# Two loads on a second queue at the head, one projection moved, and the last store in two parts

## The chip, the cores and the metric

The kernel runs as one program on one core of a Trainium2 chip. The metric is the device time of one execution in microseconds, and the trace is one profiled execution. A core has five engines that run at once, each through its own list of instructions in order: TensorE (PE in the rows, with its weight loads as PEld), VectorE (DVE), ScalarE (ACT), GpSimd (POOL) and SyncE (SP). A "q" behind a name (SPq) is the engine's sequencer, which issues the DMAs that stand in its list. The engines meet through semaphores.

## What is computed

One inference step of a one-layer hybrid encoder in fp32: 512 prompt rows and 32 sample rows of width 1024. One projection feeds three attention groups: A (chunk band with a bias), B (an indexer scores the keys, the best k are picked, attention runs over those) and M (256 memory rows).

```python
def _mixer_inputs(x, g, w_in, pos):
    z = _rmsnorm(x, g) @ w_in
    qa, ka, va, ga, qb, kb, vb, gb, qm, gm, qi, ki, wi = _split_cols(z)
...
def _merge(x, oa, ob, om, ga, gb, gm, w_out):
    o = jnp.concatenate([oa * jax.nn.silu(ga), ob * jax.nn.silu(gb), om * jax.nn.silu(gm)], axis=-1)
    return x + o @ w_out
...
y_prompt = _rmsnorm(xp, norm_final_g)
```

The columns `qi`, `ki` and `wi` (8 x 32, 32 and 8 columns: 296 together) are the indexer's queries, key and weights. The keys, values and indexer keys are outputs too.

## The kernel before

**Number form.** A prompt product is made of three fp32r products: an operand is split in a rounded part (`...h`) and the rest (`...l`), and h·h, h·l and l·h are summed in a PSUM bank. The rounded part of a weight is made by ScalarE (`rounded`), the rest by VectorE or GpSimd (`tsub`); for x the two are `xTh` (ScalarE) and `xTl` (VectorE), both scaled with the norm's weights `g_mix`. Products for the 32 sample rows take the weights as loaded (`raw`) and plain fp32 (`xF`).

**Stages.** The head is the index group: for each of 8 K tiles (128 rows of the contraction) one tile of x transposed (`xr`, 272 KB) and one tile of the 296 index columns of `w_in` (`raw`, 148 KB) are loaded, split, and multiplied (`index_group`: nine products a K tile, three token tiles each in three forms). After it come small products for the sample (`bank<-raw,xF`, which for `ka` needs all four of the 384 KB pieces of `ka`'s weights), the first key tile (`bank<-xr,gw`), and then the projections `EARLY` and `LATE` in the order of those lists, while the indexer, the picks and the attention units run between them. The end is the output projection, whose last tile is the fourth prompt tile: a squared sum, a power on GpSimd (`run`), a scale on ScalarE (columns 0 to 511) and on VectorE (columns 512 to 1023), and one store of 512 KB (`settle`).

**What sets the order.** Nothing is scheduled by hand. A planner (`Line`) is run while the kernel is written: it keeps a modelled clock per engine, costs every instruction, and starts the next step of that coroutine whose data it holds to be there. Its numbers (DMA rate by `rate`, `lag`, margins) thus set the order of the instructions on every engine. While the model says that TensorE would wait during the index group, `warm` writes filler products (`bank<-ones`, 128x128, whose result nobody reads). Every instruction of the kernel is written through one helper, so nearly all rows of the trace bear the line 405, and tiles are told apart by name.

**Names that the change touches.** `x_load` issues the loads of x and of the index weights on SP's queue. `w_split` splits the weights; `WV` lists the weight pieces (0 to 3 are the index weights, 4 to 7 those of `ka`) whose low part VectorE makes. `EARLY` orders the projections. `settle` ends a tile.

Of the kernel before, what the change touches and what calls it, by code (L numbers as in the profile page):

```python
# [10 lines left out]
F32 = mybir.dt.float32  # L11
F32R = mybir.dt.float32r
BF16 = mybir.dt.bfloat16
AF = mybir.ActivationFunctionType
ALU = mybir.AluOpType
# [3 lines left out]
P = 128  # L19
# [3 lines left out]
D = 1024  # L23
# [3 lines left out]
NT = S // P  # L27
# [8 lines left out]
WV = (0, 1, 2, 3)  # L36
# [8 lines left out]
EARLY = ("ka", "va", "mk", "mv", "qa0", "qa1", "ga0", "qa2", "ga1", "ga2", "qm0", "gm0", "qm1", "gm1")  # L45
# [15 lines left out]
class Free:  # L61


    eng = None
# [26 lines left out]

class Line:
# [4 lines left out]
    def __init__(self):  # L97
        self.clk = {"PE": 1.35, "DVE": 0.7, "ACT": 0.9, "POOL": 1.2, "SP": 0.7}
# [57 lines left out]
    @staticmethod  # L156
    def lag(of, to):

        if of is None and to == "PE":
            return 0.3  # L160
        if of == to or of is None:
            return 0.127 if to == "DVE" else 0.09 if to == "POOL" else 0.0
        return 0.95 if of == "SP" else 0.26 if to == "PE" else 0.2 if of == "PE" else 0.06 if of == "POOL" else 0.15
# [68 lines left out]
    def rate(self):  # L232

        t = self.clk["SP"]
        return 340e3 if t < 1 else 170e3 if t < 2.3 else 330e3 if t < 7 else 380e3

    def op(self, eng, op, outs, ins, kw):
# [16 lines left out]
        d = (outs[0].size() * 4 / self.rate() if eng == "SP" else  # L254
# [33 lines left out]
    def begin(self, o, t):  # L288
        last = self.last
        o.start = t  # L290
        if o.eng == "SP":
            o.end = max(t + 1.3, last["DMA"]) + o.d
            o.after = {"SP": t + 0.45, "DMA": o.end}
        else:
            d = o.d
            if o.eng == "PE":
                (self.window, self.busy, self.over, self.slow) = last["array"]
                d = self.array(t, d)
# [7 lines left out]
        self.clk[o.eng] = o.end if o.eng != "SP" else t  # L306
# [127 lines left out]
def hybrid_step(ctx: ExitStack, tc: tile.TileContext, a: dict):  # L434
    ctx.enter_context(tc.manual_schedule())
    nc = tc.nc
    line = Line()
    V, G, A, PE, DMA = (Timed(line, n, e) for n, e in (("DVE", nc.vector), ("POOL", nc.gpsimd), ("ACT", nc.scalar),
                                                       ("PE", nc.tensor), ("SP", nc.sync)))

# [94 lines left out]
    def rounded(out, in_, scale=1.0):  # L535
        A.activation(out, in_, AF.Copy, scale=scale)
# [94 lines left out]
    def w_split():  # L631
        at = {}
        for i in range(len(w_list)):
# [26 lines left out]
            if i < 4:  # L660
                for kk in range(2):
                    yield line.at(raw[:, kk, :])
                    rounded(wh[:, kk, :], raw[:, kk, :])
# [141 lines left out]
    def x_load():  # L805
# [8 lines left out]
        for kk in range(2):  # L814
# [4 lines left out]
            DMA.dma_start(raw[:, kk, :], w_in[rows, QI:QI + 296])  # L819
# [1184 lines left out]
    gf = sq = ss = None  # L2004

    def final():

        nonlocal gf, sq, ss
# [6 lines left out]
        ss = fp.tile([P, NT + 1, 8], F32, name="ss")  # L2015
        ready.append(True)
# [5 lines left out]
    def settle(t, c0, n):  # L2022
# [30 lines left out]
        A.activation(y[:rows, 0:512], y[:rows, 0:512], AF.Copy, scale=run)  # L2053
        V.scalar_tensor_tensor(y[:rows, 512:D], y[:rows, 512:D], run, gf[:rows, 512:D], op0=ALU.mult, op1=ALU.mult)
        DMA.dma_start(a["y_prompt"][t * P:(t + 1) * P, :] if t < NT else a["y_sample"], y)
# [70 lines left out]
```

## Time and profile before

| | us |
|---|---|
| median of 3 runs | 353.21 (352.42 to 353.29) |
| the profiled execution, whole | 352.53 |
| its span, first to last instruction | 350.8 |
| TensorE busy in it | 342.6 (98%) |
| VectorE, ScalarE, GpSimd busy | 277.5, 224.2, 174.3 |
| TensorE's granted clock, mean | 0.996 of full speed |

The span is what the rows cover; 1.73 us of the profiled execution lie around it. Times in the rows are microseconds from the span's start. Busy time of TensorE is taken from starts that the profiler saw and ends that it modelled: matmuls overlap in the rows, so the time of a step is read from one start to the next.

### The profile page before, as it was taken

Reading aid. Unit: us, or ns where it says so; the run is one execution under the profiler, and the core shown is the slowest. Engines: PE = TensorE matmul, PEld = TensorE weight load, DVE = VectorE, ACT = ScalarE, POOL = GpSimd, SP = SyncE. Lnnn points to the kernel's source line nnn. Section 1 sums busy time; section 2 is a strip of 40 time slices with the busy share of each in tenths; the row PEclk is TensorE's granted clock in tenths of the full one; section 3 lists DMA queues with packets and bytes.
Section 4 is the critical chain, followed back from the end, with each engine's and each line's share of the span. In section 5 each row is a group of like instructions: output and inputs, shape, how many; then the busy total and the mean of one; then the engine's idle time right before and its main releaser. Section 6 shows DMA issues by size and latency. Waiting matters only on the chain.

```text
span 350.8 us, 7580 instructions
## 1 busy us (share of the span) xinstructions
PE 342.6 (98%) x2748; PEld 300.2 (86%) x2748; DVE 277.5 (79%) x700; ACT 224.2 (64%) x536; POOL 174.3 (50%) x195
## 2 busy tenths in 40 slices
PE   8999999999999999999999999999999999999992
PEld 8979989989999998898898899899986777676882
DVE  3765768699889999997999945798996899674743
ACT  5759678898564876894757427413795786472542
POOL 3468264475554585255634473744471465215622
PEclk9999999999999999999999999999999999999998
DMA  7999542456538251343231232232372537300033
GB/s 230 323 360 354 134 140 75 143 162 152 151 92 296 66 144 39 78 127 88 76 91 45 93 124 58 60 93 98 95 284 92 180 106 265 114 0 2 0 111 143
DMA packets 39604, 46.31 MB, mean 132 GB/s; under 512 B 5360, under 2 KB 32624, under 8 KB 39568
## 3 DMA queue, kind: packets, MB, share of 16 engines
q1 hardware_dynamic: 39568, 45.85, 42.0%
q8 instruction: 21, 0.34, 0.4%
q14 instruction: 15, 0.12, 0.1%
HBM read 39.67 MB, written 6.16 MB: 131 GB/s over the span
## 4 chain that ended last, share of the span: by engine, by line
PE 95%; DVE 1%; ACT 1%; issue 1%; POOLq 0%; POOL 0%; ACTq 0%; DVEq 0%
PE bank L405 95%; DVE rot L405 1%; DVE xr L405 0%; ACT junkS L405 0%; DVE rt L405 0%; ACT wh L405 0%; ACT sq L405 0%; POOLq L2114 0%; POOL xr L405 0%; ACT bf_ok L405 0%; ACT k L405 0%; POOL ss L405 0%; ACT wI L405 0%; DVE ones L405 0%; ACTq L405 0%
## 5 line engine op out<-in xcount | busy, mean ns | idle before, releaser
L405 POOL TENSOR_TENSOR wl<-raw,wh 128x512 fp32r<-128x512 f32 (+1 forms) x69 | 104.5, 1523 | 79.9 <-ACT wh L405 68.2
L405 ACT ACTIVATE wh<-raw 128x512 fp32r<-128x512 f32 (+2 forms) x77 | 50.7, 662 | 23.4 <-PE bank L405 12.0
L405 PE MATMUL bank<-wh,xTh 128*128 128x384 f32 (+1 forms) x184 | 61.2, 347 | 0.2 <-ACT k L405 0.2
L405 PE MATMUL bank<-wl,xTh 128*128 128x384 f32 (+1 forms) x184 | 58.8, 334 | 0.0
L405 PE MATMUL bank<-wh,xTl 128*128 128x384 f32 (+1 forms) x184 | 58.5, 332 | 0.0
L405 ACT ACTIVATE z<-z,st 128x256 f32<-128x256 f32 (+3 forms) x80 | 42.4, 553 | 18.9 <-DVE st L405 18.7
L405 PE MATMUL bank<-xTh,wh 128*128 128x272 f32 x208 | 46.3, 303 | 0.0
L405 PE MATMUL bank<-xTl,wh 128*128 128x272 f32 x208 | 43.0, 288 | 0.0
L405 PE MATMUL bank<-xTh,wl 128*128 128x272 f32 x208 | 42.9, 288 | 0.0
L405 PEld LDWEIGHTS bank<-wh,xTh 128*128 128x128 f32 x184 | 34.1, 190 | 1.8 <-ACT wI L405 0.6
L405 PEld LDWEIGHTS bank<-xTh,wh 128*128 128x128 f32 x208 | 32.7, 189 | 2.7 <-issue 1.8
L405 PEld LDWEIGHTS bank<-wl,xTh 128*128 128x128 f32 x184 | 34.1, 190 | 0.0
L405 PEld LDWEIGHTS bank<-wh,xTl 128*128 128x128 f32 x184 | 33.9, 189 | 0.1
L405 PEld LDWEIGHTS bank<-xTl,wh 128*128 128x128 f32 x208 | 32.6, 188 | 0.0
L405 PEld LDWEIGHTS bank<-xTh,wl 128*128 128x128 f32 x208 | 32.6, 189 | 0.0
L405 DVE MAX8 m<-ysel 128x8 f32<-128x256 f32 (+2 forms) x48 | 26.5, 552 | 0.1
L405 DVE MATCH_REPLACE8 ysel<-m,ysel 128x256 f32<-128x256 f32 (+2 forms) x48 | 26.0, 542 | 0.0
L405 PE MATMUL bank<-ident,z 128*128 128x128 f32 (+1 forms) x162 | 24.8, 274 | 0.0
L405 ACT ACTIVATE junkS<-ysS,bi 128x1056 int8<-128x1056 f32 x16 | 18.8, 1172 | 6.8 <-DVE bi L405 5.7
L405 PEld LDWEIGHTS bank<-ident,z 128*128 128x128 f32 (+1 forms) x162 | 18.6, 140 | 5.1 <-issue 1.6
L405 ACT COPY z<-bank 128x512 f32<-128x512 f32 (+2 forms) x31 | 15.7, 520 | 10.2 <-PE bank L405 8.5
L405 DVE SCALAR_TENSOR_TENSOR ysel<-r,wI,ysel 128x256 f32<-128x256 f32 (+2 forms) x21 | 19.7, 938 | 2.4 <-ACT r L405 1.8
(299 smaller groups left out, 784.1 us busy)
## 6 DMA issues: line engine op xcount, KB each, us to landing
raw<-in_w_in_dram SPq DMA_DIRECT2D x20, 384.0 KB, 3.7
raw<-in_w_in_dram SPq DMA_DIRECT2D x26, 256.0 KB, 2.9
raw<-in_w_out_dram SPq DMA_DIRECT2D x16, 256.0 KB, 3.6
xr<-in_x_t_dram SPq DMA_DIRECT2D x8, 272.0 KB, 4.4
nat<-in_x_prompt_dram SPq DMA_DIRECT2D x4, 512.0 KB, 7.7
raw<-in_w_mem_kv_dram SPq DMA_DIRECT2D x8, 256.0 KB, 2.7
xr<-in_x_prompt_dram SPq DMA_DIRECT2D x4, 512.0 KB, 3.3
out_dram<-xr SPq DMA_DIRECT2D x4, 512.0 KB, 2.6
```

The lines of the kernel that those rows point to most:

```text
L405: return fn(*args, **kw)
```

## The change

Four edits. The loads of the index weights of the first two K tiles go on ScalarE's queue (`DMA2`), ahead of its table load, while SP goes on with x. The rounded part of the very first of them is made by VectorE. `qa0`, the first queries of group A, stands between `mk` and `mv` in `EARLY`, and the low part of `ka`'s fourth weight piece (7 in `WV`) is made by VectorE. The last prompt tile ends in two parts of 256 + 256 columns, each written to a buffer of its own (`outs`) and stored by a DMA of its own. The planner gets a clock for the new queue and another DMA rate, so its order changes elsewhere too.

```diff
-WV = (0, 1, 2, 3)
+WV = (0, 1, 2, 3, 7)
...
-EARLY = ("ka", "va", "mk", "mv", "qa0", "qa1", "ga0", "qa2", "ga1", "ga2", "qm0", "gm0", "qm1", "gm1")
+EARLY = ("ka", "va", "mk", "qa0", "mv", "qa1", "ga0", "qa2", "ga1", "ga2", "qm0", "gm0", "qm1", "gm1")
...
+QUEUES = "SP", "ACTQ"
...
-        return 340e3 if t < 1 else 170e3 if t < 2.3 else 330e3 if t < 7 else 380e3
+        return 250e3 if t < 1 else 380e3
...
+    DMA2 = Timed(line, "ACTQ", nc.scalar)
...
-                    rounded(wh[:, kk, :], raw[:, kk, :])
+                    if 2 * i + kk < 1:
+                        V.tensor_copy(wh[:, kk, :], raw[:, kk, :])
+                    else:
+                        rounded(wh[:, kk, :], raw[:, kk, :])
...
-            DMA.dma_start(raw[:, kk, :], w_in[rows, QI:QI + 296])
+            (DMA2 if c == 0 else DMA).dma_start(raw[:, kk, :], w_in[rows, QI:QI + 296])
...
+        outs = [fp.tile([P, 512], F32, name=f"out{q}") for q in range(2)]
...
-        A.activation(y[:rows, 0:512], y[:rows, 0:512], AF.Copy, scale=run)
-        V.scalar_tensor_tensor(y[:rows, 512:D], y[:rows, 512:D], run, gf[:rows, 512:D], op0=ALU.mult, op1=ALU.mult)
-        DMA.dma_start(a["y_prompt"][t * P:(t + 1) * P, :] if t < NT else a["y_sample"], y)
+        dst = a["y_prompt"][t * P:(t + 1) * P, :] if t < NT else a["y_sample"]
+
+        k = 2 if t == NT - 1 else 1
+        for q in range(k):
+            lo, hi = (slice(c + q * 512 // k, c + (q + 1) * 512 // k) for c in (0, 512))
+            out = (y if k == 1 else outs[q])[:rows].rearrange("p (h c) -> p h c", h=2)
+            A.activation(out[:, 0, :], y[:rows, lo], AF.Copy, scale=run)
+            V.scalar_tensor_tensor(out[:, 1, :], y[:rows, hi], run, gf[:rows, hi], op0=ALU.mult, op1=ALU.mult)
+            DMA.dma_start(dst.rearrange("p (h q c) -> p h q c", h=2, q=k)[:, :, q, :], out)
```

How the order moves, at three places. In these rows `xTh`, `wh` and `wl` are the split operands named above, and a number behind a name tells buffers apart.

ScalarE at the program's start, before:

```order
L405 ACT_TABLE_LOAD
L405 ACTIVATE m_75<-nhalf 128x1
L405 ACTIVATE xTh_81<-xr,g_mix 128x544
L405 ACTIVATE wh<-raw 128x296 x2
L405 ACTIVATE xTh_81<-xr,g_mix 128x544
```

ScalarE at the same place in the changed kernel:

```order
L408 DMA raw<-in_w_in_dram 128x296 x2
L408 ACT_TABLE_LOAD
L408 ACTIVATE m_75<-nhalf 128x1
L408 ACTIVATE xTh_81<-xr,g_mix 128x544 x2
L408 ACTIVATE wh<-raw 128x296
```

Two DMA issues stand ahead of the table load, one rounding of weights is gone (VectorE has it as its first work on data), and the second tile of x is split ahead of the second weights.

TensorE at the end of the index group and the start of `ka`, before:

```order
L405 MATMUL bank<-wl,xTh_82 128x296 x3
L405 MATMUL bank<-ones 128x128 x2
L405 MATMUL bank<-wh,xTl_84 128x296 x3
L405 MATMUL bank<-raw,xF 32x296 x8
L405 MATMUL bank<-xr,gw 32x128 x8
L405 MATMUL bank<-raw,xF 32x384 x8
L405 MATMUL bank<-wh,xTh_81 128x384
```

and in the changed kernel:

```order
L408 MATMUL bank<-wl,xTh_82 128x296 x3
L408 MATMUL bank<-wh,xTl_84 128x296 x3
L408 MATMUL bank<-xr,gw 32x128 x8
L408 MATMUL bank<-raw,xF 32x296 x8
L408 MATMUL bank<-raw,xF 32x384 x8
L408 MATMUL bank<-wh,xTh_81 128x384
```

The filler ahead of the last products is gone and two small products change places; the sample's product with the four pieces of `ka`'s weights (`raw,xF 32x384`) still stands ahead of `ka`'s own. Over the whole head the fillers are 17 before (10, then 3, 2 and 2) and 11 after (9 and 2); all other products of the program are the same in number and shape.

ScalarE behind the splits of the index group, before:

```order
L405 ACTIVATE wh<-raw 128x768 x2
L405 ACTIVATE wI<-bank 128x8 x3
L405 ACTIVATE wh<-raw 128x768
L405 COPY k_365<-bank 128x128
L405 COPY zS<-bank 32x296
```

and in the changed kernel:

```order
L408 ACTIVATE wh<-raw 128x768 x3
L408 ACTIVATE wI<-bank 128x8 x3
L408 COPY k_360<-bank 128x128
L408 ACTIVATE junk,ss<-nat 128x1024
L408 COPY zS<-bank 32x296
```

The copy of the first key tile (`k`) stood behind the third rounding of `ka`'s weights, and now stands right behind the three copies `wI`.

## Rows read from the trace of the kernel before

**Rows 1.** The page: TensorE's busy time, share and instructions, and the chain that ended last, by engine.

```profile
PE 342.6 (98%) x2748; PEld 300.2 (86%) x2748; DVE 277.5 (79%) x700; ACT 224.2 (64%) x536; POOL 174.3 (50%) x195
PE 95%; DVE 1%; ACT 1%; issue 1%; POOLq 0%; POOL 0%; ACTq 0%; DVEq 0%
```

**Rows 2.** Waits of TensorE from 23 to 342 us, all of them: waited for, us in total, times, the longest.

```profile
PE bank L405 <- ACT bf_ok L405: 0.7, 1, 0.7
PE bank L405 <- ACT k L405: 0.2, 1, 0.2
```

**Rows 3.** Timeline of the head: start, duration, engine, operation, and in brackets the idle time before it with its releaser.

```profile
0.72 1.28 ACT L405 ACT_TABLE_LOAD   x1 [0.72 <-PEq L2108]
0.73 0.38 SPq L405 DMA_DIRECT2D xr<-in_x_t_dram  x1
...
1.63 0.90 SPq L405 DMA_DIRECT2D raw<-in_w_in_dram  x2
...
2.57 0.43 SPq L405 DMA_DIRECT2D xr<-in_x_t_dram  x1
...
3.86 0.75 ACT L405 ACTIVATE xTh<-xr,g_mix 128x544 fp32r<-128x544 f32 x1 [1.63 <-DMA g_mix<-in_norm_mix_g_dram]
...
4.51 0.43 ACT L405 ACTIVATE wh<-raw 128x296 fp32r<-128x296 f32 x1
4.64 0.78 DVE L405 SCALAR_TENSOR_TENSOR xTl<-xr,g_mix,xTh 128x544 fp32r<-128x544 f32 x1 [3.65 <-ACT xTh L405]
...
5.33 1.09 PE L405 MATMUL bank<-wh,xTh 128*128 128x296 f32 x3
5.34 0.46 DVE L405 TENSOR_TENSOR wl<-raw,wh 128x296 fp32r<-128x296 f32 x1
...
6.60 0.75 ACT L405 ACTIVATE xTh<-xr,g_mix 128x544 fp32r<-128x544 f32 x1 [0.22 <-DMA xr<-in_x_t_dram]
...
7.35 0.83 PE L405 MATMUL bank<-ones 128*128 128x128 f32 x6
...
7.93 0.66 PE L405 MATMUL bank<-wh,xTh 128*128 128x296 f32 x3
...
10.09 0.60 PE L405 MATMUL bank<-ones 128*128 128x128 f32 x4
...
10.45 0.66 PE L405 MATMUL bank<-wh,xTl 128*128 128x296 f32 x3
```

**Rows 4.** Stretches of the head: from and to, us, busy time of each engine, the granted clock, the mean busy share of the 16 DMA engines, and GB/s.

```profile
2.50:3.50 1.00, 1.00 (x6) 1.00 (x6) 0.00 (x0) 0.00 (x0) 0.08 (x1) 1.00 0.94 271
3.50:4.50 1.00, 1.00 (x7) 1.00 (x6) 0.00 (x0) 0.64 (x1) 0.00 (x0) 1.00 0.81 182
4.50:6.50 2.00, 2.00 (x11) 2.00 (x11) 1.25 (x3) 0.90 (x3) 0.29 (x1) 1.00 0.94 316
6.50:12.00 5.50, 5.50 (x42) 5.50 (x42) 4.99 (x10) 5.27 (x10) 2.55 (x5) 1.00 1.03 374
12.00:14.00 2.00, 2.00 (x17) 2.00 (x16) 2.00 (x5) 1.68 (x4) 1.03 (x2) 1.00 1.12 209
```

**Rows 5.** The fourth piece of `ka`'s weights: its issue in SP's timeline, and in the view of DMA issues (from 13.9 to 14.4 us) its size and the time from issue to landing.

```profile
13.93 0.48 SPq L405 DMA_DIRECT2D raw<-in_w_in_dram  x1
...
raw<-in_w_in_dram SPq DMA_DIRECT2D x1, 384.0 KB, 5.8
```

**Rows 6.** Timeline of TensorE from the end of the index group into `ka`.

```profile
16.65 0.61 PE L405 MATMUL bank<-ones 128*128 128x128 f32 x4
17.01 0.65 PE L405 MATMUL bank<-wh,xTl 128*128 128x296 f32 x3
...
18.61 0.62 PE L405 MATMUL bank<-xr,gw 128*32 128x128 f32 x16
19.05 1.53 PE L405 MATMUL bank<-raw,xF 128*32 128x384 f32 x16
20.50 0.44 PE L405 MATMUL bank<-wh,xTh 128*128 128x384 f32 x1
...
22.36 0.34 PE L405 MATMUL bank<-wh,xTl 128*128 128x384 f32 x1
22.54 0.34 PE L405 MATMUL bank<-wl,xTh 128*128 128x384 f32 x1
23.04 0.44 PE L405 MATMUL bank<-wh,xTh 128*128 128x384 f32 x1 [0.17 <-ACT k L405]
```

**Rows 7.** Timeline of ScalarE at that place.

```profile
21.92 0.18 ACT L405 ACTIVATE wI<-bank 128x8 f32<-128x8 f32 x1 [1.83 <-DVE rot L405]
22.00 0.84 ACT L405 ACTIVATE wh<-raw 128x768 fp32r<-128x768 f32 x1
22.73 0.26 ACT L405 COPY k<-bank 128x128 f32<-128x128 f32 x1
```

**Rows 8.** Timeline of the end: an addition on 512 and on 256 columns, the scales, and the last store's issue.

```profile
341.78 0.69 DVE L405 TENSOR_TENSOR xr<-bank,xr 128x512 f32<-128x512 f32 x1 [1.45 <-PE bank L405]
...
343.20 0.42 DVE L405 TENSOR_TENSOR xr<-bank,xr 128x256 f32<-128x256 f32 x1
...
346.29 0.72 ACT L405 ACTIVATE xr<-xr,ss 128x512 f32<-128x512 f32 x1 [2.07 <-POOL ss L405]
346.30 0.75 DVE L405 SCALAR_TENSOR_TENSOR xr<-xr,ss,gf 128x512 f32<-128x512 f32 x1 [0.66 <-POOL ss L405]
347.11 0.33 SPq L405 DMA_DIRECT2D out_dram<-xr  x1
```

**Rows 9.** DMA issues of the whole span: stores of 512 KB and of 256 KB, with the median time to landing.

```profile
out_dram<-xr SPq DMA_DIRECT2D x4, 512.0 KB, 2.6
...
out_dram<-mk SPq DMA_DIRECT2D x1, 256.0 KB, 2.1
```

**Rows 10.** The stretch from 70 to 190 us, columns as in rows 4 (busy time of PE, PEld, DVE, ACT, POOL).

```profile
70.00:190.00 120.00, 119.30 (x1047) 109.47 (x1046) 111.16 (x328) 86.26 (x205) 66.25 (x68) 1.00 0.42 118
```

More of the change, by code (lines that the diff above doesn't have):

```diff
@@ L89, in again @@
         return When(self.of, self.by)
+QUEUES = "SP", "ACTQ"
 class Line:
     def __init__(self):
-        self.clk = {"PE": 1.35, "DVE": 0.7, "ACT": 0.9, "POOL": 1.2, "SP": 0.7}
+        self.clk = {"PE": 1.35, "DVE": 0.7, "ACT": 0.9, "POOL": 1.2, "SP": 0.7, "ACTQ": 0.7}
         self.queue = {e: deque() for e in self.clk}
@@ L162, in lag @@
             return 0.127 if to == "DVE" else 0.09 if to == "POOL" else 0.0
-        return 0.95 if of == "SP" else 0.26 if to == "PE" else 0.2 if of == "PE" else 0.06 if of == "POOL" else 0.15
+        return 0.95 if of in QUEUES else 0.26 if to == "PE" else 0.2 if of == "PE" else 0.06 if of == "POOL" else 0.15
     def box(self, x):
@@ L253, in op @@
                     deps.setdefault(o, False)
-        d = (outs[0].size() * 4 / self.rate() if eng == "SP" else
+        d = (outs[0].size() * 4 / self.rate() if eng in QUEUES else
              self.cost(eng, op, outs, ins, kw) * (1.0 if eng == "PE" else SLACK))
@@ L290, in begin @@
         o.start = t
-        if o.eng == "SP":
+        if o.eng in QUEUES:
             o.end = max(t + 1.3, last["DMA"]) + o.d
-            o.after = {"SP": t + 0.45, "DMA": o.end}
+            o.after = {o.eng: t + 0.45, "DMA": o.end}
         else:
@@ L305, in begin @@
         o.enter(last)
-        self.clk[o.eng] = o.end if o.eng != "SP" else t
+        self.clk[o.eng] = o.end if o.eng not in QUEUES else t
     def events(self):
@@ L2002, in hybrid_step @@
         line.run(out_part(AM, (c0,), lambda *_: None, [(t, c0) for t in range(NT)]))
-    gf = sq = ss = None
+    gf = sq = ss = outs = None
     def final():
-        nonlocal gf, sq, ss
+        nonlocal gf, sq, ss, outs
         yield from line.wait(lambda: 1 in over and count["done"] == len(units))
```

## The prediction

> **What bounds the kernel now.** I read the page first, then TensorE's waits, then the two ends by timeline and by stretches. The page [rows 1] says that TensorE is busy for 342.6 of 350.8 us and carries 95% of the chain that ended last. Its waits between 23 and 342 us are two, 0.7 and 0.2 us [rows 2]. So the middle, over 300 us long, is a row of products without holes, and an edit there can only add holes or close those two. The change leaves every product in place apart from six fillers less. What can be won lies where TensorE doesn't set the pace: the head, up to the place where the projections run freely (about 23 us), and the tail behind its last product.
>
> **The head: what paces it.** The first product with data starts at 5.33 [rows 3]. It needs xTh, which ScalarE makes from 3.86 on when g_mix has landed, and wh, which ScalarE makes behind it at 4.51. The second K tile's x lands only for the xTh at 6.60; SP issued it at 2.57, behind two issues of index weights that took 0.90 us together. TensorE fills the holes with ones: 7.35 to 7.93, 10.09 to 10.45 [rows 3] and 16.65 to 17.01 [rows 6], 0.58 + 0.36 + 0.36 = 1.30 us.
>
> It is tempting to count all of that as gain. But look at what follows. The sample's product with ka's weights starts at 19.05 and gives way to ka at 20.50 [rows 6]; its second half, from about 19.8, needs the third and fourth piece. The fourth was issued at 13.93 and took 5.8 us [rows 5]: it landed at 19.7. So the product of before arrives just when its data do, with no slack. TensorE can come there as early as it likes: it goes on only as much earlier as the load stream runs earlier. **The head's gain is the gain of the load stream**, not of TensorE.
>
> How much that is: the stream moves 271, 182 and 316 GB/s in the stretches from 2.5 to 6.5, and 374 from 6.5 to 12 [rows 4]. From 2.5 to 6.5 that is 271 + 182 + 2 x 316 = 1085 KB. At 374 GB/s it would take 2.9 us in place of 4.0: gain 1.1, the upper bound. But the DMA engines were busy for 0.94, 0.81 and 0.94 of those stretches; their idle share is 0.06 + 0.19 + 2 x 0.06 = 0.37 us, and if only that is filled, the gain is 0.4, the lower bound. The second x is issued where the first weights were, at 1.63 in place of 2.57, 0.94 us earlier [rows 3]. I take 0.8, near the middle and near that issue. The slow stretch from 12 to 14 us (209 GB/s) stays.
>
> Does TensorE arrive early enough to use 0.8? The fillers behind the first product fall from seven to two. Seven cost 1.30, so two some 0.4, and 0.9 us are free even if its products start no earlier. Enough, just.
>
> Edits in the head with no price of their own: the two DMA issues on ScalarE's queue have no row there; the nearest are SP's, 0.38 to 0.45 each [rows 3]. Ahead of the table load (1.28) they put its end at 0.72 + 0.90 + 1.28 = 2.9, with the first work on data at 3.86: hidden by the load of x and g_mix; at twice that price the load ends at 3.8, just in time. VectorE's rounding of the first weights has no row either; the same columns take 0.46 on VectorE and 0.43 on ScalarE, and it lies ahead of xTl (4.64), in time in which VectorE waited for 3.65 us [rows 3]. It would cost if raw landed later than xTh was made, since xTl and wl are queued behind it. A loss is possible: x and g_mix now share the DMA engines with 296 KB of weights, and at 271 GB/s that is up to 1.1 us later for the first xTh. But the bytes then come sooner for the second K tile, and the stream as a whole isn't slower, so I price it at nothing at the place that counts.
>
> **The hole at 23.04.** ka's thirteenth product starts at 23.04, where the rhythm of 0.18 us (22.36, 22.54) would have put it at 22.72: 0.32 us lost for a bank that ScalarE's copy k frees [rows 6]. That copy started at 22.73, behind a rounding of ka's weights that began at 22.00 and behind the last wI at 21.92, which waited for VectorE [rows 7]. Now the copy stands straight behind wI. If wI comes when it did, k is done by 22.4, while ka's thirteenth product comes at 22.72 - 0.8 = 21.9 and would wait; but wI waits for VectorE's work on the index group, which moves with the end of that group, at least 0.9 us earlier. So k is free at about 21.4 and the hole closes: gain 0.3, between 0 and 0.32.
>
> **The middle.** qa0 ahead of mv and the fourth low part on VectorE (0.46 x 768 / 296 = 1.2 us, from row 5.34, in a stretch where VectorE isn't the bound) move work and add none. Since the planner rewrites its order, the waits of rows 2 needn't come back, and others may come. Bounds: the 0.7 us wait is gone (gain 0.7), or one or two more of that size come (loss 0.7 to 1.4). I take 0.
>
> **The end.** The scales start at 346.29, take 0.72 and 0.75, and the store is issued at 347.11 [rows 8] and lands 2.6 us later, at 349.7 [rows 9]. In two parts: the addition takes 0.69 on 512 columns and 0.42 on 256 [rows 8], so 256 columns save 0.27; the scale on VectorE takes 0.75 - 0.27 = 0.48 on half. The first part is ready at 346.8 and issued at once (0.33). The second is ready at 346.3 + 2 x 0.48 = 347.25 at the latest, and issued at 347.3. The store of mk has its size and landed in 2.1 [rows 9]: 349.4. Gain 0.3. If the second part queues behind the first and takes 2.6, it lands at 349.9: loss 0.2. If the parts overlap on VectorE, gain 0.5.
>
> **The sum.** 0.8 + 0.3 + 0 + 0.3 = 1.4 us. Against the profiled execution's own 352.53 that is 351.1; it lay 0.68 below the median of the runs (353.21), and from there it would be 351.8. I take 351.5. Its own range, from the terms' bounds, is 350.4 to 352.6.
>
> **Rivals.** (1) *A second queue gives nothing.* The DMA engines were busy for 0.81 to 0.94 of the early stretches [rows 4]; if a packet takes its time whoever issues it, two queues share the same rate, and the stream gains 0 to 0.4, say 0.2. The total is 0.2 + 0.3 + 0.3 = 0.8: 352.4 from the median, within 0.3%. Against it: the same engines, hardly busier, moved 374 GB/s from 6.5 on. The Trainium skill (DMA: Bandwidth & Descriptors, "Issuing engines are not separate DMA queues") says that DMAs from several engines run on the same 16 DMA engines and interleave, so that a second issuer saves only the sequencer's issue time. By that rule the most that two issues can save is SP's 0.90 us, which the 0.8 does not exceed; the rows can't yet tell whether that time was the limit.
>
> (2) *Slower: VectorE becomes the bound between 70 and 190 us.* It is busy for 111.16 of those 120 us [rows 10], the time in which picks, the sample's choice and the first attention units share it. With qa0 earlier the first units' VectorE work falls on the picks. If a unit's results come later than planned, TensorE stands, as it did for bf_ok, 0.7 us a time [rows 2]. It decides from the fourth such wait on: 4 x 0.7 eats the 1.4 and another 1.1 us and more, the bound of slower; six give 353.21 - 1.4 + 4.2 = 356.0. Against it: VectorE still has 8.8 us free there, and TensorE other projections to fill with.
>
> (3) *Better: TensorE's waits all go.* The stream at its upper bound (1.1), k (0.3), bf_ok (0.7) and the end at 0.5 make 2.6: 349.9 to 350.6.
>
> (4) *The end isn't shorter*, since the second store queues behind the first: -0.2 for +0.3, total 0.9: 352.3, a tie.
>
> **How the numbers follow.** A measurement of this kernel tells about 0.3% from no change, 1.06 us: faster is below 352.15. Chances: the forecast 0.46, (3) 0.17, (1) 0.21, (4) 0.07, (2) 0.09. Faster: 0.17 and most (0.43) of the forecast's, and some of (1) and (4), 0.04: 0.64. Slower: (2), 0.09. Same: the rest, 0.27. The range goes from 349.9, case (3), to 353.4, which takes in (1) and (4) and leaves out (2) and the ends.
>
> **What would show it.** Head: ka's first product at 19.4 in place of 20.50, with TensorE standing just ahead of the second half of raw,xF: right. At 19.0 or earlier: the product didn't wait for data as I read it. At 20 or later: (1). GB/s in 3.5 to 4.5 well above 182 is the same step's other sign. k: no hole at ka's thirteenth product. End: two stores, the second landing some 3.1 us behind the start of the scales, where it was 3.4. Middle: TensorE's waits from 23 us on in sum 0 to 1.5 us; over 2.5 and behind VectorE, (2) holds. I am wrong above all if the reordered middle moves by more than the head and the end together.

## The result and the profile after

The changed kernel takes 356.90 us (median of 6 runs, 355.87 to 359.38) where before takes 352.96 in the same sessions: a ratio of 1.0118, interval 1.0094 to 1.0142. It is 1.2% slower; the forecast was 351.5 and the range ended at 353.4. The profiled execution took 357.92 with a span of 355.9, so it lies 1.0 above its median, and the traces differ by 5.1 us of span where the medians differ by 3.9.

The page of the changed kernel, TensorE's row and the chain, to be held against [rows 1]:

```profile
PE 344.4 (97%) x2736; PEld 299.9 (84%) x2736; DVE 281.8 (79%) x701; ACT 224.7 (63%) x533; POOL 179.9 (51%) x202
PE 75%; DVE 13%; DMA 5%; issue 2%; ACT 2%; POOL 2%; POOLq 0%; ACTq 0%; SPq 0%; DVEq 0%
```

TensorE still has the work, but its share of the chain fell from 95% to 75%: the chain now leaves it for VectorE and for DMAs. Most of VectorE's part is one stretch of the chain, from 159.9 to 200.2 us, that ends in a wait of 0.5 us for `kb`. TensorE's waits over the whole span (waited for, us in total, times, longest), against [rows 2]:

```profile
PE bank L408 <- DMA cache<-in_cache_b_v_dram: 2.1, 2, 2.0
...
PE bank L408 <- ACT ka L408: 0.6, 1, 0.6
PE bank L408 <- DVE kb L408: 0.5, 1, 0.5
PE bank L408 <- ACT cacheM L408: 0.5, 1, 0.5
PE bank L408 <- DMA raw<-in_w_in_dram: 0.2, 1, 0.2
```

The row left out, 1.0 us for `ones` at the program's start, is in both kernels. Before had one wait of this size behind the start, 0.7 for `bf_ok`, and it is gone. Four others took its place. The largest is for the cached values of group B (`cache`, two loads of 768 KB). TensorE at that place, and the same place in stretches (columns as in rows 4):

```profile
296.50 0.65 PE L408 MATMUL bank<-cache,ptS 128*32 128x64 f32 x32 [0.16 <-DMA cache<-in_cache_b_v_dram]
299.11 0.65 PE L408 MATMUL bank<-cache,ptS 128*32 128x64 f32 x32 [1.96 <-DMA cache<-in_cache_b_v_dram]
```

```profile
296.00:299.00 3.00, 0.99 (x34) 0.49 (x32) 1.79 (x2) 0.78 (x2) 0.91 (x1) 1.00 0.76 278
299.00:302.00 3.00, 2.89 (x55) 2.51 (x56) 0.67 (x6) 0.32 (x2) 0.00 (x0) 0.61 0.12 40
302.00:305.00 3.00, 3.00 (x17) 1.96 (x17) 1.89 (x9) 2.24 (x9) 0.00 (x0) 0.82 0.41 122
```

The kernel before comes to the same products at 297.58, waits for nothing and keeps the full clock (a line of TensorE's timeline, then two stretches):

```profile
297.58 1.10 PE L405 MATMUL bank<-cache,ptS 128*32 128x64 f32 x64
```

```profile
296.00:299.00 3.00, 3.00 (x89) 2.56 (x89) 2.95 (x13) 2.57 (x10) 1.78 (x2) 1.00 0.93 347
299.00:305.00 6.00, 6.00 (x54) 4.15 (x52) 3.60 (x12) 3.33 (x11) 1.94 (x5) 1.00 0.20 64
```

After two microseconds without products the granted clock is 0.61 and 0.82 of full speed in the next two stretches: part of that time TensorE ran at 1.2 in place of 2.4 GHz. That holds for the profiled execution. The two stretches take (0.39 + 0.18) x 3 = 1.7 us of full clock, 0.005 of the span, and the mean granted clock of this execution is 0.993. Three of the six executions (355.87, 356.22 and 357.58 us) have means of 0.997, 0.997 and 0.998, which leave no room for that, and are like before's (0.994 to 0.999). They are 2.9 to 4.6 us above before's median all the same, so the low clock isn't needed for the loss.

The loads themselves, in the view of DMA issues (of before from 290.4 to 291.2 us, of the changed kernel from 289 to 290):

```profile
cache<-in_cache_b_v_dram SPq DMA_DIRECT2D x2, 768.0 KB, 6.0
```

```profile
cache<-in_cache_b_v_dram SPq DMA_DIRECT2D x2, 768.0 KB, 8.2
```

They were issued 1.1 us earlier (289.40 for 290.54), took 2.2 us longer, and TensorE came to them 1.1 us earlier than in before (296.50 for 297.58). Just ahead of them SP had issued four 256 KB pieces of `w_out` (286.66 to 288.88), in before two (286.12 to 286.94), and from 290 to 291 us the DMA engines still moved 308 GB/s, in before 31. That fits loads that shared the engines with others in flight; no run shows it by itself.

The head, TensorE's timeline and the load stream, against [rows 4, 6]:

```profile
19.40 0.84 PE L408 MATMUL bank<-raw,xF 128*32 128x384 f32 x4 [0.24 <-DMA raw<-in_w_in_dram]
20.17 0.45 PE L408 MATMUL bank<-wh,xTh 128*128 128x384 f32 x1
...
22.37 0.34 PE L408 MATMUL bank<-wh,xTh 128*128 128x384 f32 x1
```

```profile
2.50:3.50 1.00, 1.00 (x6) 1.00 (x6) 0.00 (x0) 0.63 (x2) 0.08 (x1) 1.00 0.98 350
3.50:4.50 1.00, 1.00 (x7) 1.00 (x6) 0.29 (x1) 0.02 (x1) 0.00 (x0) 1.00 1.09 391
4.50:6.50 2.00, 1.98 (x11) 1.68 (x10) 1.26 (x4) 1.78 (x3) 0.59 (x2) 1.00 1.05 356
6.50:12.00 5.50, 5.50 (x42) 5.47 (x41) 5.22 (x10) 4.58 (x9) 1.92 (x4) 1.00 1.03 351
12.00:14.00 2.00, 2.00 (x17) 2.00 (x16) 1.96 (x5) 1.79 (x4) 0.82 (x2) 1.00 0.89 163
```

`ka` starts 0.33 us earlier (20.17 for 20.50), and its thirteenth product 0.67 earlier (22.37 for 23.04), since the hole for `k` is closed. The stream is much faster from 2.5 to 6.5 us and slower from 6.5 on; it is slower ahead of 2.5, too (36 GB/s for 59 from 0 to 2.5 us), and the first `xTh` starts at 4.48 where it started at 3.86. The 0.33 is one execution against one. Two other traces with the changed kernel's order of the head (the runs that hold the cached values for later and that fill the stand) start `ka` at 20.29 and 21.21, and the run with the end alone, with before's order, starts it at 22.04: the spread is larger than the gain.

The end, against [rows 8, 9]:

```profile
351.15 0.91 ACT L408 ACTIVATE out<-xr,ss 128x256 f32<-128x256 f32 x2 [2.06 <-POOL ss L408]
351.15 0.88 DVE L408 SCALAR_TENSOR_TENSOR out<-xr,ss,gf 128x256 f32<-128x256 f32 x2 [0.66 <-POOL ss L408]
351.70 1.27 SPq L408 DMA_DIRECT2D out_dram<-out  x2
```

From the start of the scales to the end of the span it is 4.75 us, where it was 4.51.

### The profile page after: what moved, and what is told of

Read it like the earlier page. It is cut to its first block, busy times and chain, and to the rows that moved or that the text cites. A ratio compares the mean times of both kernels' runs of the same rounds, so it can differ in the third digit from the quotient of the medians.

```text
span 355.9 us, 7552 instructions
## 1 busy us (share of the span) xinstructions
PE 344.4 (97%) x2736; PEld 299.9 (84%) x2736; DVE 281.8 (79%) x701; ACT 224.7 (63%) x533; POOL 179.9 (51%) x202
## 4 chain that ended last, share of the span: by engine, by line
PE 75%; DVE 13%; DMA 5%; issue 2%; ACT 2%; POOL 2%; POOLq 0%; ACTq 0%; SPq 0%; DVEq 0%
PE bank L408 75%; DVE ysel L408 3%; DMA cache<-in_cache_b_v_dram 3%; DVE m L408 3%; DMA mr<-in_mem_t_dram 2%; DVE z L408 1%; POOL rot L408 1%; DVE rotS L408 1%; DVE rot L408 1%; DVE rt L408 1%; DVE gate L408 1%; DVE kbS L408 0%; DVE kb L408 0%; DVE bi L408 0%; POOL wI L408 0%
## 5 line engine op out<-in xcount | busy, mean ns | idle before, releaser
L408 POOL TENSOR_TENSOR wl<-raw,wh 128x512 fp32r<-128x512 f32 (+1 forms) x68 | 102.6, 1518 | 81.4 <-ACT wh L408 78.2
L408 PE MATMUL bank<-ident,z 128*128 128x128 f32 (+1 forms) x162 | 25.6, 277 | 0.5 <-DVE kb L408 0.5
L408 PEld LDWEIGHTS bank<-ident,z 128*128 128x128 f32 (+1 forms) x162 | 19.8, 143 | 4.9 <-ACT wh L408 1.1
L408 ACT COPY z<-bank 128x384 f32<-128x384 f32 (+2 forms) x34 | 17.0, 509 | 9.1 <-PE bank L408 9.1
L408 DVE TENSOR_TENSOR xr<-bank,xr 128x512 f32<-128x512 f32 (+1 forms) x17 | 11.2, 658 | 11.1 <-PE bank L408 10.8
L408 DVE SCALAR_TENSOR_TENSOR ysel<-r,wI,ysel 128x256 f32<-128x256 f32 (+2 forms) x21 | 18.5, 882 | 1.7 <-ACT r L408 1.2
```

Of the source, the lines that this page charges most:

```text
L408: return fn(*args, **kw)
```

## The experiments

**Theory.** The head and the end move the time by tenths. What costs is the order that the planner writes for the 300 us between them, because its new numbers shift its clock: above all the stand for the cached values and the low clock behind it. **Rivals:** VectorE becomes the bound; the moved `qa0` or VectorE's extra low part costs; the second queue hurts the head; the end in two parts is a large part.

The planner's own clock can be read while it writes a kernel. It is no time of the chip, but it tells what the planner believed: in before, that the fourth piece of `ka`'s weights lands at 18.5, and in the changed kernel at 16.0. On the chip that piece moved by 0.3 us.

### One part at a time, the order of before kept

**Head alone.**

```diff
+    DMA2 = Timed(line, "SP", nc.scalar)
+    AV = Timed(line, "ACT", nc.vector)
...
+                    if 2 * i + kk < 1:
+                        AV.tensor_copy(wh[:, kk, :], raw[:, kk, :])
...
+            (DMA2 if c == 0 else DMA).dma_start(raw[:, kk, :], w_in[rows, QI:QI + 296])
```

> The kernel before with only the head's two hardware edits: the first two index weights on ScalarE's queue and the first rounding on VectorE; the planner is told nothing of it, so TensorE, GpSimd and everything behind the head keep the order of before. Theory (the head gains what its load stream gains, and the 4 us come from the reordered middle): ka's first product at 20.1 to 20.3 (20.50 before), 0.2 to 0.4 us faster than before, 352.6 to 352.8. Rival (sharing the DMA engines between two queues delays the first xTh and costs time in the head itself): at least as long as before, 353.0 to 353.6. The forecast's own term of 0.8 would give 352.2.

Measured: 353.10, ratio 1.0002 (0.9994 to 1.0011): no change. TensorE's timeline of this run:

```profile
19.05 1.47 PE L405 MATMUL bank<-raw,xF 128*32 128x384 f32 x16
20.45 0.44 PE L405 MATMUL bank<-wh,xTh 128*128 128x384 f32 x1
...
23.44 0.44 PE L405 MATMUL bank<-wh,xTh 128*128 128x384 f32 x1 [0.61 <-ACT k L405]
```

The theory's 20.1 to 20.3 was missed: the fillers stand in the order as before, so TensorE comes to the sample's product at 19.05 as it did [rows 6], and the wait for `k` grew from 0.17 to 0.61. The time is in the rival's range, but its mechanism was absent; the first product with data starts at 5.34 (5.33 before [rows 3]). TensorE waited 0.43 us for VectorE's `wl` at 6.42, and was level again at 7.35, where the fillers start in both. So the run shows that these edits cost nothing; what an earlier load stream would give it can't show, since TensorE comes no earlier.

**End alone.** The diff is that of the change (`outs`, `settle`).

> The kernel before with only the end in two parts; every order but that of the last two scales and stores is the one of before. Theory (the second store queues behind the first and its rows of 1 KB go no faster): 0.2 us longer, 353.2. Forecast's term: 0.3 shorter, 352.7. Either is near what can be told in the time; the trace decides: from the start of the scales to the end of the span 4.51 before, 4.75 by the theory, 4.2 by the forecast. Rival (the end is a large part of the 4 us): 354 or more.

Measured: 353.60, ratio 1.0011 (1.0000 to 1.0023). Its scales and stores:

```profile
347.40 0.91 ACT L405 ACTIVATE out<-xr,ss 128x256 f32<-128x256 f32 x2 [2.06 <-POOL ss L405]
347.95 1.27 SPq L405 DMA_DIRECT2D out_dram<-out  x2
```

With a span of 352.2 it is 4.80 us from the scales to the end: the theory's side. Over all runs this is sharp: from the last product's start to the end of the span it is 6.78 to 6.85 us in the six traces with two parts, and 6.46 to 6.53 in the nine with one part that end in the same way (most stand in the table below). The edit costs 0.3 us.

**The two moves alone,** with head, planner's clocks and end of before (`EARLY` and `WV` as in the change).

> The kernel before with only qa0 ahead of mv and the fourth low part of ka's weights on VectorE; head, planner's clocks and end as before. Theory (these two edits are not what costs; a new order brings some stands of its own): 352.5 to 355, first 40 us as before, with one or two waits over 0.5 us at places where before has none. Rival (VectorE becomes the bound between 70 and 190 us): 355 or more, with four or more waits behind VectorE in that stretch.

Measured: 353.64, ratio 1.0020 (1.0005 to 1.0035): 0.2% of loss. Waits of TensorE from 60 to 345 us:

```profile
PE bank L405 <- DVE z L405: 0.5, 1, 0.5
PE bank L405 <- ACT bf_ok L405: 0.2, 1, 0.2
```

The theory holds. VectorE is not the bound; in the changed kernel too TensorE's only wait from 70 to 190 us is the 0.5 for `cacheM`.

### The stand for the cached values

**Later use.**

```diff
-            yield line.sure(*cv)
+            yield line.sure(*cv) + (4.0 if mix == 1 else 0.0)
```

> The changed kernel, in which the planner holds the two loads of cached values (cache_b_v) for landed 4 us later than it did; the order is that of the changed kernel up to the place where TensorE stood for them (296.5 us), and only behind it TensorE does other work first. Theory (that stand of 2.1 us and the lower clock behind it, some 1.7 us, make most of the loss): no wait for these loads, granted clock 1.00 throughout 290 to 340, 353.0 to 354.5. Rival (the loss is spread over many small waits behind VectorE, from 40 to 200 us): 356 to 357, with other waits in its place.

Measured: 355.18, ratio 1.0086 (1.0054 to 1.0119), between the two expectations: 1.7 us of 3.9 came back, less than the theory had it. Its wait list has no `cache` row, and the stretch that had 0.61 has the full clock:

```profile
299.00:302.00 3.00, 3.00 (x29) 2.01 (x28) 2.74 (x13) 3.00 (x12) 0.42 (x1) 1.00 0.04 8
```

**Filled stand.**

```diff
+                    if mix == 1 and g0 == 0 and b == 4:
+                        for _ in range(9):
+                            nc.tensor.matmul(o_ps[:, 384:512], ident, ident, start=False, stop=False)
```

> The changed kernel with nine filler products (identity by identity, into columns of a bank that nobody reads) between the first and the second of the two loads of cached values, where TensorE stood 2.0 us at 297; the planner doesn't know of them, so every other order is that of the changed kernel. They take about as long as the stand. Theory (the stand itself costs 2 us, and the low clock behind it another 1.7): the products with the second load start as late as before, at about 299, but the granted clock stays 1.00 from 299 to 305, and the total is 1 to 1.7 us below the changed kernel, 355.2 to 356. Rival (the clock falls for another reason, or its fall costs nothing): 356.7 or more.

Measured: 358.86, ratio 1.0159 (1.0142 to 1.0177). TensorE at the place, and in stretches:

```profile
298.63 2.27 PE L1554 MATMUL bank<-ident 128*128 128x128 f32 x18
300.84 0.65 PE L408 MATMUL bank<-cache,ptS 128*32 128x64 f32 x32
```

```profile
299.00:302.00 3.00, 3.00 (x66) 2.79 (x66) 0.40 (x2) 0.72 (x3) 0.89 (x1) 1.00 0.45 168
302.00:305.00 3.00, 3.00 (x24) 1.96 (x24) 2.41 (x12) 2.14 (x8) 0.00 (x0) 1.00 0.24 73
```

As a saving it failed, and the time is on the rival's side. In the profiled execution two waits for loads of 0.7 us each, in the head and for `keysB`, brought TensorE there 1.55 us later, so that less was left to fill than the 2.2 us of the fillers, and they pushed the rest back. This trace has 356.1 us of span and the changed kernel's 355.9; why the medians lie 2.0 apart isn't shown. But it gives the price of the clock, since the same products follow: from the second load's products to the scales it is 351.34 - 300.84 = 50.50 us at full clock, and 351.15 - 299.11 = 52.04 in the changed kernel. In the changed kernel's profiled execution the low clock cost 1.54 us.

### Which of the edits writes the bad order

**Without the moves and the end; without `qa0`'s move; without the low part.** Each is the changed kernel with the edit taken back.

```diff
-EARLY = ("ka", "va", "mk", "qa0", "mv",
+EARLY = ("ka", "va", "mk", "mv", "qa0",
```

```diff
-WV = (0, 1, 2, 3, 7)
+WV = (0, 1, 2, 3)
```

> The changed kernel without the moved qa0, without the low part on VectorE and without the end in two parts: the head's edits and the planner's new clock and rate alone. Theory (any shift of the planner's clock by a few tenths writes another order, and each order has its own stands): more than the head's direct gain away from 352.6, between 353.3 and 356, with one or more waits of TensorE over 0.5 us that before doesn't have. Rival (the moved qa0 or VectorE's extra low part is what costs): 352.3 to 352.8, waits as before.

> The changed kernel with qa0 behind mv again, as before. Theory (the planner's new numbers cost, and qa0's place only picks another order): 355 to 361, between the changed kernel and the run without any of the three other edits (363.7). Rival (qa0 ahead of mv is what costs): 353 to 354.

> The changed kernel with the fourth low part of ka's weights on GpSimd again, as before. Theory: GpSimd makes that part late (three such parts took it 5.9 us in the changed kernel, from 16.5 on), so TensorE waits for it or for ka's banks between 20 and 45 us; 357 to 362. Rival (VectorE's extra work is what costs): 353 to 355, with fewer waits behind VectorE.

Measured: 363.70 (1.0301, 1.0270 to 1.0331), 364.51 (1.0319, 1.0290 to 1.0348) and 359.01 (1.0169, 1.0149 to 1.0188). Only the third fell where the theory had it; the first two are slower than it allowed. The rivals fall: with the planner's new numbers, taking either move back makes it worse. The slowest of the three stands 3.1 us for ScalarE's `z` and 1.2 for `ka`; a part of the rest is in the table below, where two of the three end late behind their last product.

**The rate alone, in before.**

```diff
-        return 340e3 if t < 1 else 170e3 if t < 2.3 else 330e3 if t < 7 else 380e3
+        return 250e3 if t < 1 else 380e3
```

> The kernel before with nothing changed but the planner's DMA rate (250e3 until its clock is at 1, then 380e3, as in the changed kernel); all loads stay on SP's queue, so the chip's load stream is that of before, while the planner believes the fourth piece of ka's weights to land at 16.0 in place of 18.5. Theory (the belief alone costs, with no hardware edit): 3 us or more slower than before, 356 to 362, with TensorE standing behind ScalarE's copies of ka near 40 us. Rival (the second queue or VectorE's extra work is needed for the loss): 353 to 354.

Measured: 358.49, ratio 1.0148 (1.0123 to 1.0174). One number of the planner, with no other edit, makes a larger loss than the whole change. It is not the same loss: here the planner itself has TensorE end 4.5 us later than in before (351.6 for 347.1, table below), in the changed kernel 2.1 us earlier. The engine was another than expected: TensorE waits 3.2 us in three times for GpSimd's `wl`, one of them here:

```profile
36.66 0.45 PE L405 MATMUL bank<-wl,xTh 128*128 128x384 f32 x1 [0.83 <-POOL wl L405]
```

**A slower rate in the changed kernel,** then with one end, then with more values.

```diff
-        return 250e3 if t < 1 else 380e3
+        return 250e3 if t < 1 else 320e3 if t < 12 else 380e3
```

> The changed kernel with one number changed: the planner's DMA rate is 320e3 instead of 380e3 until its clock is at 12, so that in its clock the fourth piece of ka's weights lands at 18.4, as in the planner of before (18.5), and not at 16.0; on the chip it landed at 19.69 before and at 19.42 after. Theory (the planner of the changed kernel believes in a head 2.5 us faster than it is, so ScalarE runs 1.5 us late against its plan where ka's banks are copied, and TensorE stands at 40.1 us): that stand of 0.75 us behind ScalarE goes, TensorE no longer waits 1.0 us for the fourth piece, and the total is 1 to 3 us below the changed kernel, 354 to 356. Rival (the rate is not the matter, every order has its stands): the stand at 40 goes or stays by chance and the total is 356 or more.

> The run with the slower rate (353.84), with one scale and one store at the end as before; all other orders are the same. Theory (the end in two parts costs 0.3 to 0.4): 353.4 to 353.6, and from the start of the scales to the end of the span 4.5 us where it was 4.76. Rival (the end in two parts gains its forecast 0.3): 354.1.

Measured: 353.84 (1.0023, 1.0009 to 1.0038) and 352.82 (0.9998, 0.9984 to 1.0011). The rate gives back 3.1 of the 3.9 us, and the waits for the cached values, for `kb`, `cacheM` and at 40 us for `ka` are gone. With one end it is as fast as before, faster than the 353.4 to 353.6 that was expected. From the last product to the end it is 6.47 where it was 6.79, the end's 0.3 as expected; the other 0.7 between these two is not the end's.

Is it that the plan's loads are now right, or just another order? For that three more rates (and one end), and two runs that keep 320e3 but change the order elsewhere:

> The run with the slower rate and one end (352.82), with 325e3 in place of 320e3. The fourth piece lands at 18.14 in the planner's clock (18.38 with 320e3), and the planner's clock ends at 342.9 (346.7). Theory A (a plan whose loads are right is followed: the chip's last product came 2.8 us ahead of the plan's end in before, 1.9 with 320e3): 348.5 to 351. Theory B (each order has its own stands, which the plan doesn't see): 351.5 to 356.

> The same with 315e3: the fourth piece at 18.62 in the planner's clock, its end at 348.1. Theory A: last product 1 to 3 us ahead of that, total 353.5 to 355.5. Theory B: anywhere from 352 to 360.

> The same with 340e3: the fourth piece at 17.48, 2 us before the chip's, the planner's end at 345.1, as in the changed kernel. Theory A (the plan is followed the less, the further its loads are from the chip's): last product behind the plan's end, total 353.5 to 356. Theory B: anywhere from 351 to 360.

> As the run with the slower rate and one end, but the planner holds one sample product (the one after that of the index columns in its list) for possible 2 us later; the order of the head is the same up to 27 us, and another order follows. The planner's own clock ends 1.2 us earlier with it (345.6 for 346.7). Theory (a plan whose loads are right is followed by the chip): 352.0 to 353.2, the first version at or below the kernel before. Rival (an order's stands on the chip have little to do with the planner's end): 353.5 or more.

> The head's edits with the planner's clocks alone (the run that took 363.7), with the rate of 320e3. Theory (the believed rate made that loss): 353 to 357, no stand of over 0.5 us between 38 and 48 us. Rival (without qa0 ahead of mv any planned order is poor; the planner's own clock ends at 350.4 here, as it did with 380e3): 359 or more.

Measured: 355.53 with 325e3 (1.0069, 1.0048 to 1.0089), 354.63 with 315e3 (1.0036, 1.0019 to 1.0054), 355.07 with 340e3 (1.0068, 1.0044 to 1.0093), 356.93 with the sample's product later (1.0114, 1.0093 to 1.0135) and 361.78 with the head's edits and the planner alone (1.0256, 1.0227 to 1.0285). The last two fell on the rival's side. The theory that a plan with true loads is followed falls: 325e3 and 315e3 differ by little, and the chip's last product starts 3.8 us behind the plan's end for one (346.70 for 342.9) and 1.2 ahead of it for the other (346.94 for 348.1). Nor is the rate all: in the order of 363.70 us, 320e3 gave back 1.9 of 10.7. With the head's edits and the planner's new queue, every order with `qa0` behind `mv` took 361.78 us or more. In two of the orders with other rates (325e3 and 340e3) TensorE again stood for the cached loads; with 325e3:

```profile
PE bank L408 <- DMA keysB<-in_cache_b_k_dram: 1.2, 1, 1.2
PE bank L408 <- DMA cache<-in_cache_b_v_dram: 0.8, 1, 0.8
```

**A late rate.** The planner is told that loads behind its clock of 200 are slower (260e3 with 320e3 ahead, 200e3 with 325e3).

```diff
-        return 250e3 if t < 1 else 320e3 if t < 12 else 380e3
+        return 250e3 if t < 1 else 320e3 if t < 12 else 380e3 if t < 200 else 260e3
```

> The run with 320e3 and one end (352.82), with the planner's rate at 260e3 in place of 380e3 once its clock is past 200: the second load of cached values then takes 7.4 us in the planner's clock (5.0 in the changed kernel), where the chip took 7.0 before and 9.2 in the changed kernel. The order up to about 200 us is that run's own. The planner's clock ends 3.4 us earlier with it, at 343.4. Theory A (loads held for as long as they take let the plan be followed): 349.5 to 352.0, a version below both kernels. Theory B (new stands that the plan doesn't see eat what it wins): 352.3 to 355, with waits over 0.5 us behind 200 that the run with 320e3 doesn't have.

> The run with 325e3 (355.53, which waited 1.2 and 0.8 us for cached keys and values), with the planner's rate at 200e3 once its clock is past 200; the planner's clock ends at 343.9. Theory A: those two waits go and nothing takes their place, 352.5 to 354.0. Theory B: other waits of 0.5 us and more come behind 200, 354.5 to 357.

Measured: 353.23 for the second (1.0011, 0.9998 to 1.0023): the two waits went, nothing came, 2.3 us less, as Theory A had it. The first took 358.83 (1.0184, 1.0162 to 1.0207), against both theories: TensorE waits no longer than 0.2 us anywhere behind 200, and its last product starts at 344.71, as early as with 320e3. But the end came 12.3 us behind it. The timeline there:

```profile
348.70 2.84 DVE L408 TENSOR_TENSOR xrS<-bank,xrS 32x512 f32<-32x512 f32 x4
348.73 0.33 SPq L408 DMA_DIRECT2D out_dram<-xr  x1
...
353.26 0.72 ACT L408 ACTIVATE xrS<-xrS,ss 32x512 f32<-32x512 f32 x1 [0.91 <-POOL ss L408]
354.06 0.33 SPq L408 DMA_DIRECT2D out_dram<-xrS  x1
```

The prompt's last store is issued at 348.73; the sample's (`xrS`), whose sums stand behind group B's cached values, 5.3 us later. The same late end is a part of four other slow runs: in each the sample's store is the last to be issued. The table has for each order the planner's clock (fourth piece, end of TensorE, issue of the last store) and the chip: the start of the last product with cached values, of the last product of all, and from there to the end of the span.

| run | median | plan: piece | plan: TensorE | plan: last store | cached, last | last product | to the end |
|---|---|---|---|---|---|---|---|
| before | 352.96 | 18.5 | 347.1 | 349.8 | 317.4 | 344.27 | 6.53 |
| changed kernel | 356.90 | 16.0 | 345.0 | 348.0 | 317.9 | 349.12 | 6.78 |
| cached values later | 355.18 | 16.0 | 345.4 | 348.4 | 320.0 | 346.06 | 6.84 |
| two moves alone | 353.64 | 18.5 | 349.4 | 352.2 | 310.3 | 344.83 | 6.47 |
| rate alone | 358.49 | 16.0 | 351.6 | 355.3 | 327.9 | 350.13 | 6.47 |
| no low part | 359.01 | 16.0 | 349.9 | 352.8 | 323.8 | 350.75 | 6.85 |
| head and planner | 363.70 | 16.0 | 350.8 | 357.3 | 338.9 | 353.44 | 8.96 |
| old `EARLY` | 364.51 | 16.0 | 351.0 | 357.7 | 339.6 | 354.11 | 9.19 |
| 320e3, one end | 352.82 | 18.4 | 346.7 | 349.5 | 312.6 | 344.73 | 6.47 |
| 320e3, sample later | 356.93 | 18.4 | 345.6 | 352.1 | 331.6 | 346.17 | 8.93 |
| 320e3, head alone | 361.78 | 18.4 | 350.4 | 357.0 | 336.1 | 350.63 | 8.97 |
| 315e3 | 354.63 | 18.6 | 348.1 | 350.9 | 312.4 | 346.94 | 6.46 |
| 325e3 | 355.53 | 18.1 | 342.9 | 345.6 | 315.5 | 346.70 | 6.50 |
| 340e3 | 355.07 | 17.5 | 345.1 | 347.8 | 315.3 | 346.52 | 6.48 |
| 320e3, late 260e3 | 358.83 | 18.4 | 343.4 | 353.2 | 333.6 | 344.71 | 12.29 |
| 325e3, late 200e3 | 353.23 | 18.1 | 343.9 | 346.7 | 321.1 | 345.42 | 6.48 |

Where the last cached product starts at 328 or earlier, the end comes 6.5 to 6.9 us behind the last product; where it starts at 331 or later, 8.9 to 12.3. TensorE's end in the plan tells little: of 342.9 to 347.1 the chip made 352.8 to 358.8. The plan's last store tells more. In the five orders that end late, the plan itself issues it 6.5 to 9.8 us behind TensorE's end, in the others 2.8 to 3.6 behind: the planner foresaw the late end, and an expectation that reads TensorE's clock alone (343.4 for the late 260e3) misses it. All nine orders whose last store the plan puts later than before's took longer than before; of the six with an earlier one, none was faster. No order here is faster than that of before.

## Why the prediction was wrong

**The step that failed is the middle.** The prediction said of it: "Since the planner rewrites its order, the waits of rows 2 needn't come back, and others may come", bounded it by -1.4 and +0.7, and took 0. It was the largest term. Its last sign of being wrong named the case: "I am wrong above all if the reordered middle moves by more than the head and the end together." The last product starts 349.12 - 344.27 = 4.85 us later although 0.67 were won by 23 us. Of this, the cached loads are 2.1, the clock behind them 1.54, the waits for `ka`, `cacheM` and `kb` 0.6 + 0.5 + 0.5, and `bf_ok` gives back 0.7: 4.5 - 0.67 = 3.9. The remaining 1.0 lies in gaps that no wait row names. This is the sum of the profiled execution, which lies 1.0 above its median; three of the six executions lack the low clock, so how the median's 3.9 is made up isn't shown part by part. The bounds were taken from one order's waits. Even these add up to more than the range says: 0.4 for the head, 0 for `k`, -1.4 for the middle and -0.2 for the end make 354.4 from the median of 353.21, where the prediction has 352.6 for its terms and 353.4 for the whole. The runs show how far one order lies from the next: 352.8 to 364.5 us, with the same products.

That the planner's order would move so far could be suspected from [rows 4]: the diff lets the planner count on 380 GB/s from its clock of 1 on, where the chip had 182 to 316 until 6.5. It thereby believed in a head 2.5 us faster, while the prediction gave the chip 0.8. ScalarE shows it in the changed kernel: the copies that free `ka`'s banks, planned at 38.9, came at 40.36, and TensorE stood for them. Being late against the plan isn't enough for a loss: with 320e3 and one end the same copy came 1.2 us late (38.14 for 36.9), and TensorE did not stand for it. ScalarE's timeline in the changed kernel:

```profile
39.62 0.83 ACT L408 ACTIVATE wh<-raw 128x768 fp32r<-128x768 f32 x1
40.36 0.56 ACT L408 ACTIVATE ka<-bank,rs 128x384 f32<-128x384 f32 x1
```

**Head, 0.8: mis-sized.** The cause was right: `ka`'s start is paced by the fourth piece, and TensorE stood for it in the sample's product (19.40, 0.24 us). `ka` gained 0.33 there, if the spread between executions lets it be called a gain. The loss that was priced at nothing came: the first `xTh` is 0.62 later (4.48 for 3.86), and to 2.5 us the stream moved 90 KB where it had moved 147. From 2.5 to 6.5 us it moved 350 + 391 + 2 x 356 = 1453 KB where it had moved 1085, but from 6.5 to 14 only 5.5 x 351 + 2 x 163 = 2257 where it had been 5.5 x 374 + 2 x 209 = 2475: all together some 90 KB ahead at 14 us, 0.25 us at 374 GB/s, below the lower bound of that step. That fits rival (1), for the head. SP issued the second x 0.94 us earlier (1.63 for 2.57), but stood before its issue at 4.20 and was 0.39 ahead at the sixth weights (5.53 for 5.92); the fourth piece landed 0.27 earlier (19.42 for 19.69). The Trainium skill (DMA: Bandwidth & Descriptors, "Issuing engines are not separate DMA queues") says that a second issuer saves only the time of the issue. The trace agrees, since no more than SP's 0.90 us of issues came of it; the head alone can't tell, because TensorE came to the product no earlier there.

**The hole at `k`, 0.3: right** in the changed kernel, 0.34 (the 0.67 less the 0.33). With the old order and the new head it grew instead, since what closes it is the place of the copy behind `wI`.

**The end, +0.3: wrong sign,** -0.3. Two terms failed. The issue was priced at 0.33 from a store of whole rows; two stores of 256 columns in two halves take 1.27 to issue. And a half-size store was priced at 2.1 to land, from `mk` (whose own store took 2.9 in the changed kernel); it takes as long as the whole one (view of DMA issues, changed kernel, 351 to 353 us; the whole one is in [rows 9]):

```profile
out_dram<-out SPq DMA_DIRECT2D x2, 256.0 KB, 2.6
```

That is rival (4), whose -0.2 was close.

**Rival (2)** gave nearly the right time (356.0) by a mechanism that isn't there: VectorE's busy time from 70 to 190 us is 111.10, as in [rows 10], and no wait behind it falls in that stretch. The nearest is one of 0.5 us, for `kb` at 200.2, where the rival wanted six of 0.7.

```profile
70.00:190.00 120.00, 119.54 (x1056) 108.61 (x1055) 111.10 (x328) 85.54 (x201) 69.70 (x74) 1.00 0.43 121
```

What is shown: the loss comes with the order that the planner writes. With the order of before kept, the head costs nothing and the end 0.3 us, and the two moves in an order of their own cost 0.2%. The planner's rate decides much of it: in the changed kernel rates of 315e3 to 340e3 until the clock of 12 gave back 1.4 to 4.1 us, of which 0.3 is the end's. Alone, in before, it makes 5.6, but by a plan that is itself longer. The stand for the cached values with its clock is the largest single part in the profiled execution; taking it out gave back 1.7 of the median's 3.9. What stays open: the rest of the median's loss, what in a plan puts the sample's last products late, and why the chip doesn't give what a shorter plan promises. That a true rate makes a good plan was tried and is not so.

## What to carry to other kernels

Where a planner writes the order, an edit to one of its numbers is an edit to every instruction behind it, and the order's own losses (here 0 to 12 us) outweigh edits of tenths: test the edit with the planner kept blind to it, and the planner's number by itself. Look in such an order first for loads that are needed as they land, and for a side chain (here 32 sample rows) that ends behind the main one; both can be read from two rows. Read the planner's clock of every engine, not TensorE's alone: the late ends stood in the plan. A stand of TensorE can be dearer than its length, by what the clock takes afterwards (here 1.54 us behind 2.0, in the profiled execution). And read the clock of the other executions before a cost that one trace shows is put down to all of them.

## What the runs showed of the hardware

- A stand of 2.0 us of TensorE was followed by a granted clock of 0.61 and 0.82 in two stretches of 3 us, 1.54 us of time; with fillers in its place the clock stayed at 1.00. Three other executions of the same kernel have no room for such a stretch in their mean clock (0.997 and 0.998).
- The same load of 768 KB took 6.0 us from issue to landing in one order and 8.2 in another (medians of two), where more loads had been issued just ahead of it.
- With the end alone changed, and so the same head as before, `ka`'s fourth piece came so late that TensorE waited 0.62 us and `ka` began 1.5 us later than in [rows 6]:

```profile
21.27 0.84 PE L405 MATMUL bank<-raw,xF 128*32 128x384 f32 x4 [0.62 <-DMA raw<-in_w_in_dram]
22.04 0.44 PE L405 MATMUL bank<-wh,xTh 128*128 128x384 f32 x1
```

- Halving a store of 512 KB into parts of 1 KB runs left its landing at 2.6 us and made each issue twice as long (0.64 for 0.33).
